# Making every low part of a split operand on VectorE instead of GpSimd, in a two-layer hybrid decoder trunk

## The chip, the cores and the metric

The kernel runs on one core of one Trainium2 chip. The metric is the device time of one execution in microseconds, as a median over runs. Before the change it is 3264.32 us (three runs, 3264.29 to 3269.77 us). The engines are TensorE (PE in the profile, with PEld for its weight loads), VectorE (DVE), ScalarE (ACT), GpSimd (POOL) and SyncE (SP, which here only issues DMAs).

## The reference, cut to what matters

The program computes a decoder trunk of two layers on 1040 tokens (16 meta tokens and a sequence of 1024) of width 1024, in float32. Layer 0 mixes tokens with a gated DeltaNet, layer 1 with an mLSTM, and each is followed by a squared-ReLU MLP of width 4096:

```python
for layer in range(DEPTH):                       # DEPTH = 2
    hn = rms_norm(h, attn_norm[layer])
    mix = gated_deltanet(hn, ...) if layer == 0 else mlstm(hn, ...)
    h = h + mix
    h = h + squared_relu_mlp(rms_norm(h, ffn_norm[layer]), ff_up[layer], ff_down[layer])
return h[:, N_META:]

def gated_deltanet(h, w_in, w_conv, ...):
    proj = h @ w_in                              # 1024 x 6176
    qkv = causal_conv_silu(qkv, w_conv)          # depthwise, 4 taps
    ...                                          # chunked delta rule, 16 heads of 128
    return o.reshape(b, t, GDN_V_DIM).astype(h.dtype) @ w_out

def squared_relu_mlp(h, w_up, w_down):
    a = jax.nn.relu(h @ w_up)
    return (a * a) @ w_down
```

## The kernel before

**Split operands.** Every dense product is made as three matmuls. An operand `x` is split into a high part `hi`, a copy of `x` in the type fp32r that ScalarE makes (a CAST in the profile), and a low part `lo = x - hi`, an elementwise subtraction. `mm3` (lines 115 to 117) then adds `whi*xhi`, `whi*xlo` and `wlo*xhi` into one PSUM bank. So each weight tile and each activation tile costs one CAST on ScalarE and one subtraction on VectorE or GpSimd, and line 117 is the matmul that needs the weight's low part.

**Where low parts are made.** `load_split` (lines 128 to 136) brings a weight tile of 128x1024 (128x768 in part of the mLSTM's output projection) with a DMA into `wraw`, casts it to `whi` (line 134) and subtracts it into `wlo` (line 135) on GpSimd. `wraw`, `whi` and `wlo` have two buffers each. It is called 248 times: for the input and output projections of both mixers and for the down projections of both MLPs. GpSimd also makes: half of the low parts of the first normalised input (`norm_in`, line 312, 10 of 20); every second one of the normalised input of the mLSTM (`apply`, line 986, 8 of 16); the low part of the first three of seven blocks of the MLP's combined input (`combine`, line 1011, 128x780, 16 times, while VectorE makes the other four blocks on line 1013); and, in the up projection, four of the seven low parts of 128x512 (`operand`, line 1064) in jobs whose flag `help` is set. These are the first three and the last two jobs of each MLP, which work on one half of the tokens, so 40 low parts in all.

**Stages.** The DeltaNet runs first (to about 1050 us): for each pair of heads a dense stream of input projections on TensorE (`ps_in`) is woven with the preparation of the pair before (`prep`: 15 steps of shuffle, multiply and subtract on VectorE, lines 621 to 623) and the recurrent scan of the one before that (`scan`: `pks`, `R`, `py`, `S`, lines 752 to 775). The projected column is read by a causal convolution on VectorE (lines 471 and 473). Then come the DeltaNet's output projection (`ps_out`), the up projection (`ps_up`, whose results VectorE adds on line 1075), the down projection (`ps_dn`, added to the residual `hT` on line 1168), the mLSTM (`ps_m`), its output projection (`ps_mo`, added on line 1606), and the second MLP. At the start of each up projection the normalised input is combined (`combine`, lines 1003 to 1013) beside the output projection and the first up jobs.

**What sets the order.** Each engine runs its own instructions strictly in one order, which is fixed when the program is built: a scheduler puts all instructions in order by their place in the program, by their dependences, by when a buffer comes free, and by its own estimate of durations. Moving an instruction from one engine to another therefore also changes the order of others. An instruction at the head of an engine's order that waits holds back all behind it.

GpSimd keeps some small work in either kernel: powers for norms (lines 298, 556, 705, 1569), masks and copies in `prep` (lines 595 to 598, 655, 665), and the history of the convolution (lines 462 and 468).

Of the kernel before, what the change touches and what calls it, by code (L numbers as in the profile page):

```python
# [7 lines left out]
F32 = mybir.dt.float32  # L8
# [116 lines left out]
    return raw.rearrange("p (a b) -> p a b", a=shape[1]) if len(shape) == 3 else raw  # L125


def load_split(c, src, shape, lo_engine=None):
    nc = c.nc
    raw = staging(c, shape)  # L130
    nc.sync.dma_start(out=raw, in_=src)
    hi = c.whl.tile(shape, F32R, tag="whi", name="whi")
    lo = c.whl.tile(shape, F32R, tag="wlo", name="wlo")
    nc.scalar.copy(hi, raw)  # L134
    (lo_engine or nc.gpsimd).tensor_tensor(lo, raw, hi.bitcast(F32), op=ALU.subtract)  # L135
    return hi, lo


# [65 lines left out]
class GDN:  # L204
# [79 lines left out]
    def norm_in(self):  # L284

        nc, c, g2 = self.nc, self.c, self.g2
        self.xh = [c.xact() for _ in range(KT // 2)]
        tags = ("AB", "AB", "V", "V", "sz")
        rows = 112
        spans = [(t0, min(rows, GL[0] - t0)) for t0 in range(0, GL[0], rows)]  # L290
        junk = g2.tile([P, D], F32, tag="sz", name="njunk", bufs=3)
        xs = [self.x_rows(t0, n, g2.tile([P, D], F32, tag=tg, name="nx", bufs=3 if tg == "sz" else 2))
              for (t0, n), tg in zip(spans, tags)]
        for (t0, n), xt in zip(spans, xs):
            ss = self.p2.tile([P, 1], F32, tag="xs1", name="xs1", bufs=len(xs))[:n]
            nc.scalar.activation(junk[:n], xt, AF.Square, accum_out=ss)
            nc.vector.tensor_scalar(ss, ss, 1.0 / D, EPS, op0=ALU.mult, op1=ALU.add)
            nc.gpsimd.tensor_tensor(ss, ss, c.mhalf[:n], op=ALU.pow)
            nc.vector.tensor_scalar(xt, xt, ss[:, 0:1], None, op0=ALU.mult)
        for (t0, n), xn in zip(spans, xs):  # L300
            ts = slice(t0, t0 + n)
            for kk in range(2):
                ks = slice(kk * 4, kk * 4 + 4)
                pn = self.pp.tile([P, 4, P], F32, tag="pp", name="pn")[:, :, :n]
                for j in range(4):
                    nc.tensor.transpose(pn[:, j], xn[:, (kk * 4 + j) * P:(kk * 4 + j + 1) * P], c.ident[:n, :n])
                xw = self.p2.tile([P, 4, rows], F32, tag="raw", name="xw")[:, :, :n]
                nc.vector.tensor_tensor(xw, pn, bc(c.attn_nw[0][:, ks], 2, n), op=ALU.mult)
                for j in range(2):
                    hi, lo = (t[:, :, ts] for t in self.xh[2 * kk + j])  # L310
                    nc.scalar.copy(hi, xw[:, 2 * j:2 * j + 2])
                    (nc.gpsimd, nc.vector)[kk].tensor_tensor(lo, xw[:, 2 * j:2 * j + 2], hi.bitcast(F32),
                                                             op=ALU.subtract)

    def h_init(self, cc):

# [606 lines left out]
class Norm:  # L923
# [46 lines left out]
    def apply(self, hf, pool):  # L970

        nc, c = self.nc, self.c
        self.x[hf] = []
        yield
        yield
        r = yield from self.rms(hf)
        ts = slice(hf * HALF, (hf + 1) * HALF)
        for k in range(KT):
            xn = self.pool.tile([P, HALF], F32, tag="xn", name="nxn", bufs=2)
            nc.vector.scalar_tensor_tensor(xn, c.hT[:, k, ts], self.nw[:, k:k + 1],  # L980
                                           r.rearrange("p a b -> p (a b)"), op0=ALU.mult, op1=ALU.mult)
            if k % 2 == 0:
                self.x[hf].append(pair(pool))
            hi, lo = (x[:, k % 2] for x in self.x[hf][-1])
            nc.scalar.copy(hi, xn)
            (nc.vector, nc.gpsimd)[k % 2].tensor_tensor(lo, xn, hi.bitcast(F32), op=ALU.subtract)
            yield

    def combine(self, hf, pool):

        nc, c = self.nc, self.c
        self.x[hf] = []
        yield
        yield
        r = yield from self.rms(hf)
        ts = slice(hf * HALF, (hf + 1) * HALF)
        for j in range(KT // 2):
            b, t = (x.rearrange("p (a b) -> p a b", b=G) for x in self.stages())  # L1000
            hi, lo = (pool.tile([P, 7, G], F32R, tag=n, name=n) for n in ("xhi", "xlo"))
            for k, out in ((j, b[:, 0:4:3]), (j + 4, b[:, 1:3])):
                nc.vector.scalar_tensor_tensor(out, c.hT[:, k, ts].rearrange("p (a b) -> p a b", b=G),  # L1003
                                               self.nw[:, k:k + 1], r, op0=ALU.mult, op1=ALU.mult)
            nc.vector.tensor_tensor(t[:, 0], b[:, 3], b[:, 0], op=ALU.subtract)
            nc.vector.tensor_tensor(t[:, 2], b[:, 2], b[:, 3], op=ALU.subtract)
            nc.vector.tensor_tensor(t[:, 1], b[:, 2], t[:, 0], op=ALU.subtract)
            nc.vector.tensor_tensor(t[:, 3], b[:, 1], t[:, 1], op=ALU.subtract)  # L1008
            yield
            nc.scalar.copy(hi[:, 0:3], b[:, 0:3])  # L1010
            nc.gpsimd.tensor_tensor(lo[:, 0:3], b[:, 0:3], hi[:, 0:3].bitcast(F32), op=ALU.subtract)  # L1011
            nc.scalar.copy(hi[:, 3:7], t)
            nc.vector.tensor_tensor(lo[:, 3:7], t, hi[:, 3:7].bitcast(F32), op=ALU.subtract)
            self.x[hf].append((hi, lo))
            yield


class Up:
# [17 lines left out]
        nc.sync.dma_start(out=r2, in_=w[:, :, (2 * i + 1) * P:(2 * i + 2) * P])  # L1036
        return r1, r2

    def operand(self, raw, name, help):

        nc, c = self.nc, self.c
        r1, r2 = raw[:2]
        a11, a12, a21, a22 = r1[:, 0:4], r1[:, 4:8], r2[:, 0:4], r2[:, 4:8]

        def sub(out, a, b, op=ALU.subtract):
            nc.vector.tensor_tensor(out, a, b, op=op)  # L1046
            return out
        if name == "s2":
            s3 = self.u1.tile([P, KT // 2, P], F32, tag="s3", name="s3")
            raw.append(sub(s3, a11, a21))  # L1050
            x = sub(a11, a22, s3)
        elif name == "s3":
            x = raw[2]
        elif name == "s1":
            x = sub(a21, a21, a22, ALU.add)
        elif name == "s4":
            x = sub(a12, a12, a11)
        else:
            x = {"a11": a11, "a12": a12, "a22": a22}[name]
        w = c.whl.tile([P, KT, P], F32R, tag=("whi", "wlo")[self.nop % 2], name="uop")  # L1060
        self.nop += 1
        nc.scalar.copy(w[:, 0:4], x)  # L1062
        lo = nc.gpsimd if help and name in ("a12", "s3", "a22", "s4") else nc.vector
        lo.tensor_tensor(w[:, 4:8], x, w[:, 0:4].bitcast(F32), op=ALU.subtract)  # L1064
        return w

    def evac(self, i, hs, name, ps, tmp):
# [33 lines left out]
    def run(self, jobs):  # L1101
# [1 line left out]
        n, ahead = len(self.ORDER), 3  # L1103
        raws, ops = {0: list(self.load(jobs[0][0]))}, {}
        done = 0
        for ji, (i, parts, help, before) in enumerate(jobs):
            if before:
                before()
            hs = slice(parts[0], parts[-1] + 1)
            tmp = {}  # L1110
            for u, (name, xi) in enumerate(self.ORDER):
                while done <= min(ji * n + u + ahead, len(jobs) * n - 1):
                    dj, du = divmod(done, n)
                    ops[done] = self.operand(raws[dj], self.ORDER[du][0], jobs[dj][2])
                    if du == n - 1 and dj + 1 < len(jobs):
                        raws[dj + 1] = list(self.load(jobs[dj + 1][0]))
                    done += 1
                w = ops.pop(ji * n + u)
                ps = self.ps.tile([P, 2, 512], F32, tag="pu", name="ps_up")[:, :, :G]
                for hf in parts:  # L1120
                    for k in range(4):
                        hi, lo = (x[:, xi] for x in self.norm.x[hf][k])
                        mm3(self.nc, ps[:, hf], w[:, k], w[:, 4 + k], hi, lo, k == 0, k == 3)
                    yield
                self.evac(i, hs, name, ps[:, hs], tmp)
# [62 lines left out]
def mlp(c, w_up, w_down, norm, spans, sides, xa, st, acts, after, closed):  # L1188
# [5 lines left out]
    with ExitStack() as ust:  # L1194
# [3 lines left out]
        def first_done():  # L1198
# [3 lines left out]
            down.fetch(0)  # L1202
            for j in range(HB):
                down.load(j)
        jobs = [(i, (0,), True, None) for i in range(e)]
        for i in range(e, n - 2):
            jobs.append((i, (0, 1), False, c.drain if i == e else None))
            if i < 2 * e:
                jobs.append((i - e, (1,), False, None))
            elif i < 2 * e + 2:  # L1210
                jobs.append((n - 2 + i - 2 * e, (0,), False, None))
        jobs += [(i, (1,), True, first_done if i == n - 2 else None) for i in range(n - 2, n)]
        c.weave(up.run(jobs))
    down.open(st, sides[0])
    c.norm_psum(True)
# [541 lines left out]
```

## Time and profile before

| | before |
|---|---|
| median of 3 runs | 3264.32 us |
| the profiled execution | 3269.28 us |
| its span, first to last instruction | 3267.5 us |
| TensorE busy | 3095.0 us (95%) |
| VectorE busy | 1910.2 us (58%) |
| ScalarE busy | 1480.2 us (45%) |
| GpSimd busy | 983.4 us (30%) |
| mean granted TensorE clock | 0.984 of full speed |

Busy times of engines overlap each other; each row is to be read against the span. A busy TensorE is one with a matmul in flight, whether at full pace or not. The difference between its busy time and the span is time in which no matmul was in flight.

### The profile page before, as it was taken

The numbers are of one execution on the slowest core, as the hardware profiler recorded it, in microseconds if no ns is written. First come the engines' busy times: TensorE is split into PE (matmuls) and PEld (weight loads), VectorE is DVE, ScalarE is ACT, GpSimd is POOL, SyncE is SP. The second block draws the span as 40 slices with busy tenths as digits, with TensorE's granted clock in tenths as the row PEclk, the third lists the DMA queues.
The fourth block names the chain that finished last, engine by engine and source line by source line (L and its number), as shares of the span: only waits on it lengthen the run. The fifth ranks groups of instructions, "written<-read, shape, count | busy, mean of one in ns | idle before, by whom it ended". The sixth has DMA issues, their size and how long they took to land. (4 is left out here: it accounts for less than half of the span.)

```text
span 3267.5 us, 66042 instructions
## 1 busy us (share of the span) xinstructions
PE 3095.0 (95%) x26788; PEld 2933.6 (90%) x26788; DVE 1910.2 (58%) x4161; ACT 1480.2 (45%) x3394; POOL 983.4 (30%) x858
## 2 busy tenths in 40 slices
PE   7899999998999997999999998999998899999999
PEld 6888888888889897899999998988897799989998
DVE  6767778777766458776634437223237976553332
ACT  5666666665555433555511114444334555441112
POOL 4544554454444334100222224211124300022222
PEclk9899999999999998999999999999998999999999
DMA  3223223322324642433523322221122244343323
GB/s 98 75 75 88 70 80 88 88 82 76 88 67 134 206 141 73 124 120 116 161 73 98 98 66 72 60 59 51 49 91 72 82 137 123 108 132 98 104 85 97
DMA packets 402224, 311.00 MB, mean 95 GB/s; under 512 B 30175, under 2 KB 366432, under 8 KB 401920
## 3 DMA queue, kind: packets, MB, share of 16 engines
q1 hardware_dynamic: 366320, 272.69, 28.5%
q10 hardware_dynamic: 35600, 34.10, 3.0%
q8 instruction: 211, 3.46, 0.4%
q14 instruction: 93, 0.76, 0.1%
HBM read 248.11 MB, written 58.62 MB: 94 GB/s over the span
## 5 line engine op out<-in xcount | busy, mean ns | idle before, releaser
L135 POOL TENSOR_TENSOR wlo<-wraw,whi 128x1024 fp32r<-128x1024 f32 (+1 forms) x248 | 599.3, 2417 | 1163.4 <-ACT whi L134 1123.6
L115 PE MATMUL ps_up<-xhi,uop 128*128 128x260 f32 x1792 | 512.5, 286 | 27.5 <-ACT uop L1062 8.8
L115 PE MATMUL ps_dn<-act_hi,whi 128*128 128x260 f32 (+1 forms) x1792 | 534.7, 299 | 1.8 <-DVE hT L1168 1.6
L116 PE MATMUL ps_dn<-act_lo,whi 128*128 128x260 f32 (+1 forms) x1792 | 534.6, 298 | 0.0
L117 PE MATMUL ps_dn<-act_hi,wlo 128*128 128x260 f32 (+1 forms) x1792 | 532.0, 298 | 0.1
L117 PE MATMUL ps_up<-xhi,uop 128*128 128x260 f32 x1792 | 510.2, 285 | 8.1 <-DVE uop L1064 7.8
L116 PE MATMUL ps_up<-xlo,uop 128*128 128x260 f32 x1792 | 511.3, 286 | 0.2 <-POOL xlo L1011 0.2
L115 PE MATMUL ps_in<-act_hi,whi 128*128 128x264 f32 (+1 forms) x1536 | 457.1, 298 | 20.2 <-ACT raw L465 12.4
L134 ACT CAST whi<-wraw 128x1024 fp32r<-128x1024 f32 (+1 forms) x248 | 255.9, 1032 | 480.2 <-PE ps_dn L116 361.6
L116 PE MATMUL ps_in<-act_lo,whi 128*128 128x264 f32 (+1 forms) x1536 | 453.0, 295 | 0.0
L1168 DVE TENSOR_TENSOR hT<-hT,ps_dn 128x260 f32<-128x260 f32 (+1 forms) x448 | 204.8, 461 | 424.1 <-PE ps_dn L117 423.7
L117 PE MATMUL ps_in<-act_hi,wlo 128*128 128x264 f32 (+1 forms) x1536 | 451.1, 294 | 0.0
L115 PEld LDWEIGHTS ps_up<-xhi,uop 128*128 128x128 f32 x1792 | 342.6, 191 | 31.9 <-ACT uop L1062 12.5
L117 PEld LDWEIGHTS ps_up<-xhi,uop 128*128 128x128 f32 x1792 | 342.2, 191 | 9.6 <-DVE uop L1064 8.8
L115 PEld LDWEIGHTS ps_dn<-act_hi,whi 128*128 128x128 f32 x1792 | 336.9, 188 | 13.8 <-issue 1.4
L117 PEld LDWEIGHTS ps_dn<-act_hi,wlo 128*128 128x128 f32 x1792 | 337.4, 189 | 11.0 <-POOL wlo L135 0.3
L116 PEld LDWEIGHTS ps_dn<-act_lo,whi 128*128 128x128 f32 x1792 | 337.1, 188 | 10.4
L116 PEld LDWEIGHTS ps_up<-xlo,uop 128*128 128x128 f32 x1792 | 342.6, 191 | 0.5 <-POOL xlo L1011 0.4
L115 PEld LDWEIGHTS ps_in<-act_hi,whi 128*128 128x128 f32 x1536 | 294.5, 192 | 26.3 <-ACT raw L465 14.1
L117 PEld LDWEIGHTS ps_in<-act_hi,wlo 128*128 128x128 f32 x1536 | 294.5, 192 | 4.3 <-issue 1.6
L116 PEld LDWEIGHTS ps_in<-act_lo,whi 128*128 128x128 f32 x1536 | 294.6, 192 | 3.8 <-issue 1.4
L115 PE MATMUL ps_m<-act_hi,whi 128*128 128x260 f32 x768 | 224.2, 292 | 6.8 <-ACT mso L1444 3.7
(419 smaller groups left out, 6845.3 us busy)
## 6 DMA issues: line engine op xcount, KB each, us to landing
wraw<-in_gdn_in_dram SPq DMA_DIRECT2D x96, 512.0 KB
wraw<-in_ff_down_dram SPq DMA_DIRECT2D x72, 512.0 KB
a_st<-d_a SPq DMA_DIRECT2D x64, 520.0 KB
d_a<-up_c ACTq DMA_DIRECT2D x88, 260.0 KB
wraw<-in_ff_up_dram SPq DMA_DIRECT2D x42, 512.0 KB
r<-in_ff_up_dram SPq DMA_DIRECT2D x42, 512.0 KB
wraw<-in_gdn_out_dram SPq DMA_DIRECT2D x32, 512.0 KB
wraw<-in_mlstm_in_dram SPq DMA_DIRECT2D x28, 512.0 KB
```

What stands on the lines that cost most here:

```text
L115: nc.tensor.matmul(ps, whi, xhi, start=first, stop=False)
L116: nc.tensor.matmul(ps, whi, xlo, start=False, stop=False)
L117: nc.tensor.matmul(ps, wlo, xhi, start=False, stop=last)
L134: nc.scalar.copy(hi, raw)
L135: (lo_engine or nc.gpsimd).tensor_tensor(lo, raw, hi.bitcast(F32), op=ALU.subtract)
L1168: nc.vector.tensor_tensor(hT[:, d, t0:t0 + n], hT[:, d, t0:t0 + n], ps, op=ALU.add)
```

## The change

Every low part is subtracted on VectorE. The parameter `lo_engine`, the alternation of engines in `norm_in` and `apply`, and the flag `help` go; GpSimd keeps its small work. 322 subtractions move.

```diff
-def load_split(c, src, shape, lo_engine=None):
+def load_split(c, src, shape):
...
     nc.scalar.copy(hi, raw)
-    (lo_engine or nc.gpsimd).tensor_tensor(lo, raw, hi.bitcast(F32), op=ALU.subtract)
+    nc.vector.tensor_tensor(lo, raw, hi.bitcast(F32), op=ALU.subtract)
     return hi, lo
...
-                    (nc.gpsimd, nc.vector)[kk].tensor_tensor(lo, xw[:, 2 * j:2 * j + 2], hi.bitcast(F32),
-                                                             op=ALU.subtract)
+                    nc.vector.tensor_tensor(lo, xw[:, 2 * j:2 * j + 2], hi.bitcast(F32), op=ALU.subtract)
...
-            (nc.vector, nc.gpsimd)[k % 2].tensor_tensor(lo, xn, hi.bitcast(F32), op=ALU.subtract)
+            nc.vector.tensor_tensor(lo, xn, hi.bitcast(F32), op=ALU.subtract)
...
-            nc.gpsimd.tensor_tensor(lo[:, 0:3], b[:, 0:3], hi[:, 0:3].bitcast(F32), op=ALU.subtract)
+            nc.vector.tensor_tensor(lo[:, 0:3], b[:, 0:3], hi[:, 0:3].bitcast(F32), op=ALU.subtract)
...
-        lo = nc.gpsimd if help and name in ("a12", "s3", "a22", "s4") else nc.vector
-        lo.tensor_tensor(w[:, 4:8], x, w[:, 0:4].bitcast(F32), op=ALU.subtract)
+        nc.vector.tensor_tensor(w[:, 4:8], x, w[:, 0:4].bitcast(F32), op=ALU.subtract)
```

VectorE's order at the start of the DeltaNet, where the input is normalised (`nx`), transposed by TensorE (`pn`), scaled into `xw` and split, and where the first two weight tiles are split. Before:

```order
28 L312 TENSOR_TENSOR act_lo<-xw,act_hi 128x2x112 x2
29 L299 TENSOR_SCALAR nx<-nx,xs_212 80x1024
30 L308 TENSOR_TENSOR xw<-pn,ncols 128x448 x2
31 L312 TENSOR_TENSOR act_lo<-xw,act_hi 128x2x112 x2
32 L308 TENSOR_TENSOR xw<-pn,ncols 128x448 x2
```

and now:

```order
28 L312 TENSOR_TENSOR act_lo<-xw,act_hi 128x2x112 x3
29 L299 TENSOR_SCALAR nx<-nx,xs_212 80x1024
30 L312 TENSOR_TENSOR act_lo<-xw,act_hi 128x2x112
31 L308 TENSOR_TENSOR xw<-pn,ncols 128x448
32 L135 TENSOR_TENSOR wlo<-wraw,whi 128x1024
33 L308 TENSOR_TENSOR xw<-pn,ncols 128x448
34 L135 TENSOR_TENSOR wlo<-wraw,whi 128x1024
35 L312 TENSOR_TENSOR act_lo<-xw,act_hi 128x2x112 x4
36 L308 TENSOR_TENSOR xw<-pn,ncols 128x448 x2
```

The two weight tiles' low parts now stand behind line 299 and around the second `xw`, and each `xw` is followed by four low parts where two stood.

VectorE's order in the mLSTM's output projection, where `combine` for the second MLP runs beside it (`st_b`, `st_t` and `xlo` are `combine`'s, `hT<-hT,ps_mo` frees a PSUM bank of the projection). Before:

```order
2518 L1606 TENSOR_TENSOR hT<-hT,ps_mo 128x260
2519 L1005 TENSOR_TENSOR st_t<-st_b 128x260
2520 L1006 TENSOR_TENSOR st_t<-st_b 128x260
2521 L1007 TENSOR_TENSOR st_t<-st_b,st_t 128x260
2522 L1008 TENSOR_TENSOR st_t<-st_b,st_t 128x260
2523 L1606 TENSOR_TENSOR hT<-hT,ps_mo 128x260
```

and now:

```order
2781 L1604 TENSOR_TENSOR hT<-hT,ps_mo 128x260
2782 L1010 TENSOR_TENSOR xlo<-st_b,xhi 128x780
2783 L1004 TENSOR_TENSOR st_t<-st_b 128x260
2784 L1005 TENSOR_TENSOR st_t<-st_b 128x260
2785 L135 TENSOR_TENSOR wlo<-wraw,whi 128x768
2786 L1604 TENSOR_TENSOR hT<-hT,ps_mo 128x260
2787 L1006 TENSOR_TENSOR st_t<-st_b,st_t 128x260
2788 L1007 TENSOR_TENSOR st_t<-st_b,st_t 128x260
2789 L1604 TENSOR_TENSOR hT<-hT,ps_mo 128x260
```

Between two additions to `hT` there now stand the low part of `combine` and that of a weight tile, and two of `combine`'s own steps have moved behind the second addition.

## Rows read from the trace of the kernel before

**Rows 1.** The page: span; busy us, share and count by engine
```profile
span 3267.5 us, 66042 instructions
PE 3095.0 (95%) x26788; PEld 2933.6 (90%) x26788; DVE 1910.2 (58%) x4161; ACT 1480.2 (45%) x3394; POOL 983.4 (30%) x858
```

**Rows 2.** Windows by stage: length, then each engine's busy us, granted clock, DMA
```profile
0.00:1100.00 1100.00, 1013.16 (x10733) 940.58 (x10734) 791.71 (x2200) 654.68 (x1869) 511.29 (x632) 0.98 0.31 88
1100.00:1350.00 250.00, 216.23 (x1663) 209.50 (x1662) 168.86 (x238) 103.95 (x194) 93.09 (x46) 0.95 0.42 130
1600.00:1950.00 350.00, 347.42 (x2885) 346.79 (x2885) 144.21 (x281) 76.26 (x95) 88.17 (x40) 1.00 0.31 99
1950.00:2050.00 100.00, 89.80 (x711) 86.76 (x710) 66.09 (x86) 40.36 (x80) 46.24 (x24) 0.97 0.25 70
2450.00:2600.00 150.00, 125.61 (x877) 116.81 (x877) 128.35 (x217) 69.89 (x148) 59.88 (x32) 0.90 0.25 75
```

**Rows 3.** Waits of TensorE: who for whom, us in total, times, longest
```profile
PE pks L752 <- DVE S L771: 17.3, 22, 2.3
PE pn L306 <- DVE xw L308: 12.6, 3, 9.9
...
PE ps_out L117 <- POOL wlo L135: 1.6, 2, 1.4
```

**Rows 4.** Costliest groups by line: count, busy us, mean ns, idle before
```profile
L135 POOL TENSOR_TENSOR wlo<-wraw,whi 128x1024 fp32r<-128x1024 f32 (+1 forms) x248 | 599.3, 2417 | 1163.4 <-ACT whi L134 1123.6 <-PE ps_mo L117 14.7 <-PE mpo L1541 7.4
...
L471 DVE TENSOR_SCALAR acc<-raw,ncols 128x528 f32<-128x528 f32 (+1 forms) x64 | 99.6, 1556 | 45.0 <-ACT raw L465 44.7
```

**Rows 5.** Groups of VectorE by shape: busy us, mean ns, idle before
```profile
L1149 DVE TENSOR_TENSOR act_lo<-a_st,act_hi 128x1040 fp32r<-128x1040 f32 x64 | 78.6, 1245 | 17.2 <-ACT act_hi L1148 16.9
...
L1005 DVE TENSOR_TENSOR st_t<-st_b 128x260 f32<-128x260 f32 x16 | 20.2, 1261 | 0.0
```

**Rows 6.** Single lines of VectorE: durations in ns as min/median/max
```profile
L471 DVE TENSOR_SCALAR acc<-raw,ncols x64: 472/1801/2721, 40.6 to 998.0; 128x528 f32<-128x528 f32 x32, 128x512 f32<-128x512 f32 x32
L941 DVE TENSOR_TENSOR ss<-ss,nsq x84: 415/430/2620, 1174.5 to 2547.4; 128x260 f32<-128x260 f32 x84
L1005 DVE TENSOR_TENSOR st_t<-st_b x16: 416/1340/2634, 1224.8 to 2598.8; 128x260 f32<-128x260 f32 x16
L1064 DVE TENSOR_TENSOR uop<-r,uop x74: 677/693/1764, 1281.9 to 2886.2; 128x512 fp32r<-128x512 f32 x74
L1168 DVE TENSOR_TENSOR hT<-hT,ps_dn x448: 410/426/681, 1626.7 to 3261.0; 128x260 f32<-128x260 f32 x148, 128x504 f32<-128x504 f32 x2
```

**Rows 7.** Timeline at the DeltaNet's start: start us, duration us, [idle before]
```profile
15.83 0.75 DVE L299 TENSOR_SCALAR nx<-nx,xs 112x1024 f32<-112x1024 f32 x1
...
18.04 5.74 DVE L299 TENSOR_SCALAR nx<-nx,xs 80x1024 f32<-80x1024 f32 x1
18.60 4.63 POOL L135 TENSOR_TENSOR wlo<-wraw,whi 128x1024 fp32r<-128x1024 f32 x2
...
24.37 1.75 PE L306 MATMUL pn<-ident,nx 112*128 112x112 f32 x8 [9.92 <-DVE xw L308]
```

**Rows 8.** Timeline in the mLSTM's output projection
```profile
2521.51 2.93 POOL L135 TENSOR_TENSOR wlo<-wraw,whi 128x1024 fp32r<-128x1024 f32 x1 [3.21 <-ACT whi L134]
...
2522.47 2.26 DVE L1005 TENSOR_TENSOR st_t<-st_b 128x260 f32<-128x260 f32 x1
2524.41 2.01 POOL L1011 TENSOR_TENSOR xlo<-st_b,xhi 128x780 fp32r<-128x780 f32 x1
2524.66 2.05 DVE L1006 TENSOR_TENSOR st_t<-st_b 128x260 f32<-128x260 f32 x1
...
2527.43 0.59 PE L115 MATMUL ps_mo<-act_hi,whi 128*128 128x260 f32 x1 [4.32 <-DVE hT L1606]
```

**Rows 9.** All waits: VectorE behind ScalarE's casts and copies
```profile
DVE uop L1064 <- ACT uop L1062: 51.8, 55, 2.7
...
DVE acc L471 <- ACT raw L465: 44.7, 32, 3.7
```

More of the change, by code (lines that the diff above doesn't have):

```diff
@@ L1037, in load, with operand @@
         return r1, r2
-    def operand(self, raw, name, help):
+    def operand(self, raw, name):
         nc, c = self.nc, self.c
@@ L1105, in run @@
         done = 0
-        for ji, (i, parts, help, before) in enumerate(jobs):
+        for ji, (i, parts, before) in enumerate(jobs):
             if before:
@@ L1113, in run @@
                     dj, du = divmod(done, n)
-                    ops[done] = self.operand(raws[dj], self.ORDER[du][0], jobs[dj][2])
+                    ops[done] = self.operand(raws[dj], self.ORDER[du][0])
                     if du == n - 1 and dj + 1 < len(jobs):
@@ L1204, in first_done @@
                 down.load(j)
-        jobs = [(i, (0,), True, None) for i in range(e)]
+        jobs = [(i, (0,), None) for i in range(e)]
         for i in range(e, n - 2):
-            jobs.append((i, (0, 1), False, c.drain if i == e else None))
+            jobs.append((i, (0, 1), c.drain if i == e else None))
             if i < 2 * e:
-                jobs.append((i - e, (1,), False, None))
+                jobs.append((i - e, (1,), None))
             elif i < 2 * e + 2:
-                jobs.append((n - 2 + i - 2 * e, (0,), False, None))
-        jobs += [(i, (1,), True, first_done if i == n - 2 else None) for i in range(n - 2, n)]
+                jobs.append((n - 2 + i - 2 * e, (0,), None))
+        jobs += [(i, (1,), first_done if i == n - 2 else None) for i in range(n - 2, n)]
         c.weave(up.run(jobs))
```

## The prediction, made before the changed kernel ran

> **What bounds the kernel now.** I read the page first, then the busy times by stage, then TensorE's waits, then VectorE's instructions by shape and a few stretches of the timeline. The page shows TensorE with a matmul in flight for 3095.0 of 3267.5 us [rows 1], so TensorE is the bound, and all that the other engines can give is the 172.5 us in which it had none, plus what its clock loses. The stages differ [rows 2]. In the first down projection (1600 to 1950 us) TensorE lacks 2.6 us of 350: nothing that VectorE or GpSimd does there matters. TensorE lacks 86.8 us in the DeltaNet (0 to 1100 us), 33.8 in its output projection and the start of the first MLP (to 1350 us), 10.2 between 1950 and 2050 us, and 24.4 between 2450 and 2600 us: 155 of the 172.5 us. In these four stretches the granted clock is also a mix of its two levels, 1.2 and 2.4 GHz: 0.98, 0.95, 0.97 and 0.90 of full speed, which is 22 + 12.5 + 3 + 15 = 52 us of full-speed time. So the question is what TensorE waits for in these four.
>
> It hardly waits for GpSimd: the longest such total is 1.6 us, for weights' low parts [rows 3], though these take 2417 ns each, 599.3 us in all [rows 4]. GpSimd made them early and stood idle 1163.4 us before them. The totals at the head of the list name VectorE (`S` of the scan, 17.3 us; `xw`, 12.6 us) [rows 3]. And VectorE is slow in a way that its shapes do not explain. Line 471, one pass over 512 or 528 elements, takes 1556 ns in the mean, but 472 ns at best and 1801 in the median [rows 4, 6]. Line 941 has a median of 430 ns and a maximum of 2620; line 1005 a minimum of 416 and a median of 1340 [rows 6]. Line 1168, which reads one operand from PSUM, never exceeds 681 ns over 448 instructions [rows 6], although it runs beside GpSimd's low parts in the down projection. The timeline shows what a stretched instruction stands beside: at 18.04 us one of VectorE lasts 5.74 us, while GpSimd makes two low parts in 4.63 us, and ends just behind them [rows 7]; at 2522.47 and 2524.66 us two of 260 elements last 2.26 and 2.05 us, each until a low part on GpSimd ends [rows 8]. VectorE's instructions that read SBUF alone are held while GpSimd subtracts.
>
> **The change part by part: VectorE's account.** Added: 232 low parts of 1024 columns, 16 of 768, 40 of 512, 16 of 780, 8 of 520 and 10 of up to 224. VectorE already makes such subtractions: 1245 ns for 1040 columns [rows 5], 693 for 512 [rows 6], so on a straight line about 1.05 ns a column: 1.23, 0.96, 0.69, 0.97, 0.70 and 0.4 us. That is 285 + 15 + 28 + 16 + 6 + 4 = 353 us. Given back: what GpSimd's subtractions hold. For line 471, 99.6 us less 64 times 0.48 is 69 us [rows 4, 6]; for line 1005, 20.2 less 16 times 0.42 is 13.5 us [rows 5, 6]. The same subtraction over all of VectorE's shapes, each against its own fast tenth (the first in size is line 471's; one with almost nothing is line 1168's, with some 230 between), gives 332 us, of which about 250 fall before 1350 us, 27 between 1950 and 2050 and 36 between 2450 and 2600. The low parts that move into these stretches cost 176, 23 and 27 us there. Of GpSimd's work some stays beside VectorE, so a part of the 332 us stays as well. Its bounds: all goes, or only the share that weights' low parts have of GpSimd's busy time, 599.3 of 983.4, which is 0.61 [rows 1, 4]; I take nine tenths, 300 us, since what stays is short. So VectorE's total comes to 1910 + 353 - 300 = 1963 us, little more than before, but it moves: VectorE gets some 50 us lighter before 1350 us (225 less 176), keeps its load between 1950 and 2050, loses 5 us of it between 2450 and 2600, and gets heavier, by about 5 us in 50, in the down projections. There it is busy 144 of 350 us [rows 2], and TensorE covers it.
>
> **The two places of the order.** At the start, line 299 needs 0.75 us, as the instruction of the same line and length before it took, in place of 5.74; `xw`, for which TensorE waits 9.92 us [rows 7], then stands behind line 299, one more low part and, for its second half, one of a weight (1.23 us): I count 3 to 5 us off the wait, and 2 of these lost again to the extra low parts that follow (six of 0.4 us). In the mLSTM's output projection, between two additions to `hT` stood 2.26 + 2.05 + 0.42 us [rows 8]; now 0.97 + 0.42 + 0.42 + 0.96 = 2.8 us. Of 4.32 us of wait about 1.5 to 2 go. So even where a stretched instruction ends the wait, the new low parts take back half of what is won.
>
> **The sum.** It is made against the profiled execution, 3269.3 us, whose span is 3267.5 us; that execution is 5 us above the median of the runs. First term: TensorE's idle 155 us in the four stretches. The lower bound of what goes is nothing (the new low parts delay as much as the old stretching did), the upper about two fifths (nearly every wait that ends with a stretched instruction of VectorE or with ScalarE behind one). At the two places above a third to a half goes, but most of the waits are short and not of this kind, so I take a fifth: 31 us. Second term, the clock: the granted clock is below full speed in the stretches where TensorE waited, and at 1.00 in the down projection [rows 2]; bounds nothing and two fifths of 52 us; with a fifth of the waits I take a fifth, 10 us. Third term, the new waits of VectorE behind a `whi` that ScalarE has not yet cast, with what is queued behind: the additions that free PSUM, `S` and `R` of the scan. The bounds are nothing and the second rival's price; I take 5 us. The queues of SP are not in the change; a `wraw` buffer comes free earlier by the 1.2 us that VectorE is faster, or later where VectorE is behind, and I count it as nothing: its cover is the second buffer, and without it a late weight would show as TensorE waiting on line 115 for `whi`. The sum is 31 + 10 - 5 = 36 us less: 3233 against the profiled execution, and 3228 us against the median.
>
> A rule that speaks against the change: the Trainium skill, Perfetto Trace Analysis, section Optimizing Scalar/DVE Operations, says that with a saturated DVE it may make sense to offload work, even to GPSIMD, though it adds that the two share an SBUF port and that this might not help. By its first half the sum for 2450 to 2600 us would be a loss; it is the third rival below. By its second half the sum stands, and the stretched rows of this trace [rows 6, 8] are on that side.
>
> **The rivals.** *More comes back.* Once VectorE is on time, ScalarE's copies are too, and the scan's steps come earlier one after the other. Then two fifths of both terms: 62 + 21 - 5 = 78 us, 3187 us. For it: VectorE's own totals are only the head of TensorE's list, and line 465, on ScalarE, shares its queue with activations that wait for the convolution. Against it: many waits are of `S`, 17.3 us in 22 pieces [rows 3], where the recurrence itself is the reason.
>
> *No gain.* VectorE's total is unchanged, and one delay of 1.2 us takes the place of another. Then the time stays within 6.5 us, the 0.2% about which a measurement of this kernel can tell from no change: 3264 us.
>
> *VectorE waits at the head of its order (slower).* GpSimd could wait for `whi` at no price: 1123.6 us [rows 4]. VectorE cannot: its order is strict. The place is the DeltaNet with its output projection, where 128 of the 248 weight tiles are split (96 and 32 by the code) and VectorE is busy 72% of the time (791.71 of 1100) [rows 2]. The nearest rows: line 1064 behind its cast costs 51.8 us over the 254 low parts that VectorE makes there (42 jobs of seven, less 40), 0.20 us each; line 471 behind `raw` 44.7 us over 64, 0.70 us each [rows 9]. At 0.20 the 128 cost 26 us of VectorE's time, less than the 50 that it wins; at 0.70 they cost 90, which is 40 more. It decides from about 0.4 us each. At the upper end TensorE pays perhaps half of the 40 us, VectorE having 28% of its time free there: 20 us more, 3285 us.
>
> *VectorE becomes the bound (slower).* Between 2450 and 2600 us it is busy 128.35 of 150 us [rows 2]. If the port gave nothing back, the 27 us that move in would make 155, and the stretch 5 us longer, and likewise at the start of the first MLP: 3274 us. Against it: lines 1005 and 941, both in this stretch, are the most stretched of all [rows 6].
>
> **How the numbers follow.** The forecast has 0.55, with a range of its own from 3205 to 3250 us; more gain 0.20; no change 0.11; waits at the head 0.10; the bound 0.04. Faster by over 0.2%: 0.75; within: 0.11; slower: 0.14. The range reaches down to the first rival's 3187 and up past the unchanged 3264, and leaves out what is beyond: 3185 to 3268 us.
>
> **What would show it.** Right: line 471 near 480 ns and line 941 near 430 in the mean, VectorE's busy total within 60 us of 1963, GpSimd's under 384 us (983.4 less 599.3), TensorE's idle time in the four stretches down by about 30 us, fewer stretches at the lower clock, and the down projections unchanged in length. Wrong: a long total of VectorE's line 135 waiting for `whi`, `S` or `hT` later than before, or TensorE waiting at line 117 for `wlo`. Were VectorE's stretching to stay without GpSimd's subtractions, the whole account would fall.

## The result, and the profile after

The changed kernel takes 3133.99 us (median of 4 runs, 3129.67 to 3140.2), the kernel before 3265.16 us beside it. The ratio is 0.9597, with a 95% interval of 0.9578 to 0.9616: 131 us faster, where the prediction said 36 and its range began at 3185. The profiled execution takes 3135.46 us. Lines after the first edits have moved by one or two: 471 is 470, 941 is 940, 1005 is 1004, 1168 is 1166, 1606 is 1604.

The page after, span and busy time by engine, against [rows 1]:

```profile
span 3133.5 us, 65556 instructions
PE 3056.0 (98%) x26788; PEld 2910.6 (93%) x26788; DVE 1944.4 (62%) x4483; ACT 1482.9 (47%) x3390; POOL 303.6 (10%) x536
```

The span is 134.0 us shorter. Of these, 95.0 are time with no matmul in flight (172.5 before, 77.5 now), and 39 are time with one in flight. The mean granted clock rose from 0.984 to 0.990 of full speed; taken as what is missing to 1 times the span, the clock's loss fell from 52 us to 31. VectorE's total is 34 us higher than before, and yet TensorE waits less for it.

To see where, both kernels are cut at the same events: the last `ps_in` matmul, the first `ps_up`, `ps_dn`, `ps_m`, `ps_mo`, and so on. Windows of before: length, then busy us (count) of PE, PEld, DVE, ACT and POOL, granted clock, DMA share, GB/s. The stages are the DeltaNet, its output projection, the first down projection and the mLSTM's output projection:

```profile
0.00:1011.80 1011.80, 928.46 (x9725) 862.20 (x9726) 744.58 (x2053) 611.88 (x1743) 474.73 (x592) 0.98 0.30 82
1011.80:1272.10 260.30, 239.93 (x2217) 229.32 (x2216) 148.79 (x287) 107.68 (x243) 104.12 (x71) 0.96 0.48 148
...
1623.70:1998.40 374.70, 371.17 (x3095) 369.91 (x3094) 161.45 (x310) 78.29 (x101) 92.67 (x41) 1.00 0.28 88
...
2395.40:2541.70 146.30, 134.13 (x967) 121.33 (x966) 93.55 (x185) 56.59 (x131) 52.65 (x26) 0.93 0.24 71
```

The same four stages after:

```profile
0.00:925.80 925.80, 899.98 (x9703) 846.10 (x9704) 691.17 (x2127) 609.27 (x1730) 266.06 (x484) 0.99 0.32 90
925.80:1160.50 234.70, 228.86 (x2215) 221.58 (x2214) 150.09 (x351) 108.91 (x249) 20.56 (x36) 0.99 0.52 164
...
1514.30:1883.50 369.20, 368.93 (x3080) 368.61 (x3081) 189.16 (x348) 77.85 (x101) 0.16 (x1) 1.00 0.28 88
...
2275.60:2413.70 138.10, 132.84 (x975) 119.31 (x974) 94.61 (x208) 56.81 (x131) 4.21 (x2) 0.96 0.25 75
```

The DeltaNet gives 86.0 of the 134 us, its output projection 25.6, the mLSTM's output projection 8.2, the other stages 14 together. In the DeltaNet TensorE's idle time falls from 83.3 to 25.8 us. The cuts are made where the next stage's matmuls begin, and after the change two stages overlap: the first `ps_up` runs 3.2 us before the last `ps_out`, the first `ps_m` 1.8 us before the last `ps_dn`. From first to last matmul the output projection is 22.1 us shorter, the first down projection 3.6.

Waits of TensorE (us in total, times, longest). Two of before that [rows 3] does not show:

```profile
PE ps_in L115 <- ACT raw L465: 12.4, 8, 3.6
PE py L722 <- DVE R L757: 11.3, 13, 1.5
```

After, against these and [rows 3]:

```profile
PE pn L306 <- DVE xw L308: 8.6, 4, 5.1
PE ps_up L115 <- DVE up_u L1073: 7.8, 6, 2.2
PE ps_up L117 <- DVE uop L1062: 6.6, 6, 2.0
...
PE ps_mo L115 <- DVE hT L1604: 2.9, 4, 1.1
...
PE pks L751 <- DVE S L770: 1.5, 1, 1.5
```

The wait for the scan's `S`, 17.3 us before, is 1.5 us; that for `raw` is 1.0, and that for `R` is gone. Added up, the waits behind VectorE fell from 104.9 us (90 waits) to 45.4 (44), those behind ScalarE from 52.2 to 19.8. No wait for `wlo` has come in.

Lines of VectorE: first the two of [rows 4] (count, busy us, mean ns, idle before), then single lines against [rows 6] (min/median/max ns):

```profile
L135 DVE TENSOR_TENSOR wlo<-wraw,whi 128x1024 fp32r<-128x1024 f32 (+1 forms) x248 | 299.9, 1209 | 149.3 <-ACT whi L134 146.8 <-ACT o L744 0.9 <-PE po L753 0.7
...
L470 DVE TENSOR_SCALAR acc<-raw,ncols 128x528 f32<-128x528 f32 (+1 forms) x64 | 32.9, 514 | 1.2 <-ACT raw L464 1.2
```

```profile
L470 DVE TENSOR_SCALAR acc<-raw,ncols x64: 475/487/687, 37.2 to 913.3; 128x528 f32<-128x528 f32 x32, 128x512 f32<-128x512 f32 x32
L940 DVE TENSOR_TENSOR ss<-ss,nsq x84: 412/422/432, 1080.0 to 2426.4; 128x260 f32<-128x260 f32 x84
L1004 DVE TENSOR_TENSOR st_t<-st_b x16: 414/421/425, 1132.4 to 2466.7; 128x260 f32<-128x260 f32 x16
```

The convolution's first pass took 1556 ns in the mean and takes 514; the maxima of 2620 and 2634 ns of the other two are 432 and 425. Most of the stretch is gone: by the prediction's measure, each instruction against its shape's fast tenth, VectorE had 331 us of it and has 48. In its place VectorE has 299.9 us of weights' low parts, and waits 146.8 us for `whi` at the head of its order, 136 times; 60.3 us of that, in 55 waits, lie in the DeltaNet and its output projection. The wait of the convolution for `raw`, 44.7 us [rows 9], is 1.2.

The two places of the order. The start (start us, duration us, [idle before]), against [rows 7]:

```profile
17.29 0.75 DVE L299 TENSOR_SCALAR nx<-nx,xs 80x1024 f32<-80x1024 f32 x1 [0.44 <-POOL xs L298]
17.96 0.38 DVE L312 TENSOR_TENSOR act_lo<-xw,act_hi 128x224 fp32r<-128x224 f32 x1
18.26 0.61 DVE L308 TENSOR_TENSOR xw<-pn,ncols 128x448 f32<-128x448 f32 x1
...
18.93 1.01 PE L306 MATMUL pn<-ident,nx 112*128 112x112 f32 x4 [5.12 <-DVE xw L308]
```

Line 299 takes 0.75 us in place of 5.74, and TensorE's wait is 5.12 us in place of 9.92. The mLSTM's output projection, against [rows 8]:

```profile
2384.02 0.42 DVE L1604 TENSOR_TENSOR hT<-hT,ps_mo 128x260 f32<-128x260 f32 x1
...
2386.72 0.42 DVE L1004 TENSOR_TENSOR st_t<-st_b 128x260 f32<-128x260 f32 x1
...
2387.06 0.42 DVE L1005 TENSOR_TENSOR st_t<-st_b 128x260 f32<-128x260 f32 x1
...
2387.40 0.95 DVE L135 TENSOR_TENSOR wlo<-wraw,whi 128x768 fp32r<-128x768 f32 x1
...
2388.27 0.41 DVE L1604 TENSOR_TENSOR hT<-hT,ps_mo 128x260 f32<-128x260 f32 x1
```

The two steps of 2.26 and 2.05 us take 0.42 each; the longest wait for `hT` there is 1.1 us, not 4.32.

### The profile page after: what moved, and what is told of

Its sections match the earlier page's. It is cut to its first block, busy times and chain, and to the rows that moved or that the text cites. A ratio compares the mean times of both kernels' runs of the same rounds, so it can differ in the third digit from the quotient of the medians.

```text
span 3133.5 us, 65556 instructions
## 1 busy us (share of the span) xinstructions
PE 3056.0 (98%) x26788; PEld 2910.6 (93%) x26788; DVE 1944.4 (62%) x4483; ACT 1482.9 (47%) x3390; POOL 303.6 (10%) x536
## 4 chain that ended last, share of the span: by engine, by line
PE 83%; DVE 7%; DMA 5%; ACT 2%; issue 1%; POOL 1%; SPq 0%; POOLq 0%; DVEq 0%; ACTq 0%
PE ps_dn L115 8%; PE ps_dn L116 8%; PE ps_dn L117 8%; PE ps_up L115 5%; PE ps_up L116 5%; PE ps_up L117 5%; PE ps_in L115 5%; PE ps_in L117 5%; PE ps_in L116 5%; PE ps_m L115 3%; PE ps_m L117 3%; PE ps_m L116 3%; PE ps_out L115 2%; PE ps_out L117 2%; PE ps_out L116 2%
## 5 line engine op out<-in xcount | busy, mean ns | idle before, releaser
L116 PE MATMUL ps_in<-act_lo,whi 128*128 128x264 f32 (+1 forms) x1536 | 446.7, 291 | 0.0
L135 DVE TENSOR_TENSOR wlo<-wraw,whi 128x1024 fp32r<-128x1024 f32 (+1 forms) x248 | 299.9, 1209 | 149.3 <-ACT whi L134 146.8
```

What stands on the lines that cost most here:

```text
L116: nc.tensor.matmul(ps, whi, xlo, start=False, stop=False)
L135: nc.vector.tensor_tensor(lo, raw, hi.bitcast(F32), op=ALU.subtract)
```

## The experiments

Each kernel has four runs, taken beside seven of the kernel before (medians of 3264 to 3268 us). "DeltaNet" is the length of that stage in the profiled execution, to the last `ps_in` matmul (before 1011.8, after 925.8), and VectorE its busy time there. Each kernel that adds to the 96 weight tiles of the DeltaNet's input projection does so in `load_w`.

**Which part of the change gives it.** e3_gdn_only is the kernel before with only the low parts of the DeltaNet's input and of the 96 tiles on VectorE; e4_rest_only is the rest of the change alone.

```
-        return load_split(self.c, ..., [P, KT, P])
+        return load_split(self.c, ..., [P, KT, P], self.nc.vector)     # e3, on before
+        return load_split(self.c, ..., [P, KT, P], self.nc.gpsimd)     # e4, on after
```

> The kernel before, with only the low parts of the DeltaNet's input (10) and of its 96 input projection tiles moved to VectorE. Theory A: the DeltaNet's stretch as short as in the changed kernel (about 926 us to the last matmul of its input projections, 86 less than before), the rest as before: 3179 us. Theory B: not less than 3230 us unless the order in that stretch is the cause; if it is, also 3179. The prediction's share (a fifth of the idle time): 3245 us.

> The changed kernel, with only the low parts of the DeltaNet's input and of its 96 input projection tiles back on GpSimd. Theory A: 3217 us, the 48 us that the other stages won, with the DeltaNet's stretch at 1012 us. Theory B: no forecast, since the order differs from both; somewhere between 3134 and 3265. If the two partial changes do not add up to the whole (86 + 48 of 134), something passes from one stage to the other.

e3 takes 3181.61 us (ratio 0.9750, 0.9734 to 0.9766), DeltaNet 925.1; e4 3215.54 us (0.9849, 0.9834 to 0.9864), DeltaNet 1009.6. Both come out as expected. The gains of 85 and 51 us add up to 136, against 131 to 134 for both, so the stages can be studied apart; the following runs change the DeltaNet alone.

**Holds put back.** e1_port, e6_one and e7_eighths are the kernel after with a GpSimd subtraction per tile that nobody reads, of the same 1024 columns in two pieces, in one, and in eight (in one piece the unread result is bf16, in the others float32); e2_queue fills GpSimd's time and reads one column per tile.

```
+    def hold(self, hi):                       # called for each tile
+        h, pool = hi.rearrange("p a b -> p (a b)").bitcast(F32), self.nc.gpsimd
+        for a in (0, 512):                    # e1; e7: range(0, 1024, 128); e6: all at once
+            pool.tensor_tensor(self.scratch, h[:, a:a + 512], h[:, a:a + 512], op=ALU.subtract)
...
+        pool.tensor_copy(self.scratch[:, 0:1], h[:, 0:1])      # e2 in place of these
+        for _ in range(4):
+            pool.memset(self.scratch, 0.0)
```

> The changed kernel, and for each of the 96 weight tiles of the DeltaNet's input projections GpSimd also makes two subtractions of 128x512 of the tile's high part from itself, into a scratch tile that nobody reads. VectorE still makes every low part that is used. Theory A (VectorE's instructions are held while GpSimd reads SBUF): line 470 goes back above 1500 ns in the mean, and the DeltaNet's stretch loses at least the 86 us that it won: 3220 us or more, up to 3290, since VectorE now has both the low parts and the stretching. Theory B (the new order that the scheduler made is the gain): within 15 us of the changed kernel, 3134 us. Theory C (GpSimd's small work no longer queues behind 2.4 us subtractions): about 3200 to 3220 us, as GpSimd's queue is as full as before, but with line 470 near 500 ns.

> As the kernel with the two extra subtractions on GpSimd, but in their place a copy of one column and four memsets of 128x512, about 2.1 us on GpSimd for each of the 96 tiles, which only write. Theory A: at most 20 us above the changed kernel (3134 to 3155 us), with line 470 well under 1000 ns. Theory B: 3134 us within 15. Theory C: about 3200 to 3220 us, as with the subtractions.

> As e1, with one GpSimd subtraction of 128x1024 (hi - hi, in a scratch tile that nobody reads) per DeltaNet weight tile, where e1 had two of 128x512: the same elements, half as many instructions, each twice as long. Theory 'a hold lasts as long as the GpSimd instruction': the convolution's scalar line goes from 815 ns in e1 towards the 1556 of before, and the time rises above e1's 3198, to about 3220. Rival 'the number of elements on GpSimd decides, not the length of a piece': the line stays near 815 ns and the time near 3198.

> As e1, with eight GpSimd subtractions of 128x128 per DeltaNet weight tile in place of two of 128x512: the same elements again, in pieces of a quarter of the length. Theory 'a hold lasts as long as the GpSimd instruction': the convolution's scalar line at 500 to 650 ns, and the time near that of e2, 3145 to 3165. Rival 'the elements decide': near e1's, 815 ns and 3198; many short holds in a row would look the same as a long one.

| | us | ratio, interval | DeltaNet us | VectorE us |
|---|---|---|---|---|
| after | 3133.99 | 0.9597, 0.9578 to 0.9616 | 925.8 | 691.2 |
| e2_queue | 3144.84 | 0.9633, 0.9619 to 0.9648 | 935.1 | 685.3 |
| e7_eighths | 3170.84 | 0.9707, 0.9691 to 0.9724 | 968.4 | 735.5 |
| e1_port | 3198.37 | 0.9797, 0.9774 to 0.9819 | 989.0 | 791.6 |
| e6_one | 3220.45 | 0.9861, 0.9846 to 0.9876 | 1015.0 | 814.8 |

The convolution's first pass (min/median/max ns) in e7, in e1 and in e6:

```profile
L478 DVE TENSOR_SCALAR acc<-raw,ncols x64: 474/610/716, 37.2 to 942.4; 128x528 f32<-128x528 f32 x32, 128x512 f32<-128x512 f32 x32
```

```profile
L478 DVE TENSOR_SCALAR acc<-raw,ncols x64: 472/682/1354, 37.6 to 969.1; 128x528 f32<-128x528 f32 x32, 128x512 f32<-128x512 f32 x32
```

```profile
L477 DVE TENSOR_SCALAR acc<-raw,ncols x64: 473/486/2129, 38.0 to 988.6; 128x528 f32<-128x528 f32 x32, 128x512 f32<-128x512 f32 x32
```

And the GpSimd instruction beside it in each, in the same order:

```profile
L450 POOL TENSOR_TENSOR scratch<-whi x768: 390/402/5573, 17.5 to 945.6; 128x128 f32<-128x128 f32 x192
```

```profile
L450 POOL TENSOR_TENSOR scratch<-whi x192: 1029/1068/6215, 17.5 to 968.2; 128x512 f32<-128x512 f32 x192
```

```profile
L449 POOL TENSOR_TENSOR scratch<-whi x96: 1883/2157/7067, 17.0 to 987.7; 128x1024 bf16<-128x1024 f32 x96
```

The longest pass grows with the GpSimd instruction: 716, 1354 and 2129 ns beside 402, 1068 and 2157 in the median. In e6 43 of the 64 passes stay under 700 ns and the other 21 last over 1500, with none between: a pass is held for long or hardly at all. The Trainium skill, SBUF — State Buffer, section "SBUF: two separate sides", says that the port pair which the two engines share is locked by one of them for the whole instruction, and is not split; these rows agree. The same elements in longer instructions cost more time, 37, 64 and 86 us over after, so the rival of e6 and e7 ("the elements decide") falls. So does another, that the added reads keep the buffers of `whi` busy: ScalarE waits for them 4.8 us in e7, 2.8 in e1 and 2.1 in e6. e2, whose GpSimd is busy for 525 us of the stage (e1: 523), costs only 11, and some of its passes are held too (up to 956 ns, as the last section shows for longer fills): GpSimd's crowded order is a small part. Three sizes were missed: e1 was expected at 3220 us or more with a pass above 1500 ns in the mean (815), and e7 came out 6 us above its interval.

**Work put on VectorE.** e5_twice subtracts each tile's low part twice; e8_aside and e10_half add an unread subtraction on VectorE, at every tile and at every second; e9_before_aside is e8's edit on the kernel before; e11_no_lo has no low part for these tiles (left out of the result: the third matmul reads the high part).

```
+        for _ in range(2):                                                    # e5
+            nc.vector.tensor_tensor(lo, raw, hi.bitcast(F32), op=ALU.subtract)
...
+        self.nc.vector.tensor_tensor(self.scratch, h, h, op=ALU.subtract)     # e8, e9; e10: if col // P % 2
...
+        self.nc.scalar.copy(hi, raw)                                          # e11
+        return hi, hi
```

> The kernel after, with the low part of each of the 96 weight tiles of the DeltaNet's input projection subtracted twice on VectorE, into the same tile: 96 x 1.23 = 118 us more of VectorE's work in the DeltaNet, none of it stretched and all of it known to the scheduler. It tests why the gain was 131 us where 36 were forecast. Theory 'planned work is cheap': 122 us of low parts that the change adds there cost little, because TensorE has other work in the order at such a place; e1 gave 63 us of time for 100 us of stretch (0.63), which with about 175 us of stretch before and 86 us of gain leaves about 0.2 us of time for each us of planned work. Then +24 us: about 3158. Rival 'a us of VectorE is a us of VectorE': a planned us costs as much as a stretched one, 0.63: +74 us, about 3208; then the gain would have another cause than the stretch.

> The kernel after, with one more VectorE subtraction of 128x1024 per DeltaNet weight tile that nobody reads (hi - hi into a scratch tile), beside the low part and not in it: as much extra work as in e5 (96 x 1.2 = 115 us), but off the path of the low part. e5 measured +67 us where the cheap-work theory said +24. Theory 'work on VectorE costs about 0.6 us of time for each us, whatever it is' (then stretch and low parts count alike, and some 50 us of the gain in the DeltaNet must come from something else than VectorE's load): +65 to +75 us, about 3200. Theory 'planned work is cheap, e5's price was the late low part': 0 to +25 us, about 3150.

> The kernel before, with the same unread VectorE subtraction of 128x1024 per DeltaNet weight tile: VectorE gets the work that the change brings it there (96 x 1.2 = 115 us), and GpSimd goes on making the low parts. Theory 'a us is a us': about +70 us, 3335. Theory 'planned work is cheap': +0 to +25, 3265 to 3290. e6, which has VectorE's low parts and as long holds as before, came to 1015 us in the DeltaNet against 1012 before; if e9 costs 70, then making the low part on GpSimd costs some 50 to 70 us by itself, beside the stretch; if it costs nothing, the stretch alone explains before.

> As e8, with the unread VectorE subtraction at every second DeltaNet weight tile only: 48 x 1.2 = 58 us more of VectorE's work than after. e8's 115 us cost 92. Theory 'VectorE's planned work is cheap while the order has room for it and dear beyond' (own work of VectorE in the DeltaNet, unstretched and summed: 751 us after, 862 in e5 and e8; v1 with 819 was no slower than after): +5 to +25 us, 3140 to 3160. Theory 'every us of VectorE costs the same 0.7 to 0.8': +41 to +46, about 3178.

> The kernel after without the 96 low parts of the weights of the DeltaNet's input projection: the third matmul takes the high part again in place of the low part, so as many matmuls run, and 96 x 1.23 = 118 us of VectorE's work go (the low parts of these weights are left out of the result). It measures what the added low parts cost the change in that stage. Theory 'cheap while there is room': 0 to 15 us less than after, 3120 to 3134, and the term that the prediction subtracted for new low parts was far too large. Theory 'every us costs the same': 0.7 x 118 = 83 us less by rate, cut off where TensorE's own 895 us of that stage bind, so 25 to 30 us less, about 3105.

| | us | ratio, interval | DeltaNet us | VectorE us |
|---|---|---|---|---|
| e11_no_lo | 3129.00 | 0.9575, 0.9556 to 0.9594 | 923.4 | 589.0 |
| after | 3133.99 | 0.9597, 0.9578 to 0.9616 | 925.8 | 691.2 |
| e10_half | 3156.57 | 0.9664, 0.9643 to 0.9685 | 954.4 | 732.2 |
| e5_twice | 3200.66 | 0.9804, 0.9790 to 0.9819 | 994.7 | 783.7 |
| e8_aside | 3226.42 | 0.9884, 0.9869 to 0.9899 | 1011.9 | 783.9 |
| before | 3264 to 3268 | 1 | 1011.8 | 744.6 |
| e9_before_aside | 3308.44 | 1.0144, 1.0123 to 1.0165 | 1056.6 | 861.8 |

e5 broke the theory that I had drawn from e1 (work that stands in the order is cheap): 67 us where it said 24. e8 showed that it was not the late low part, since the work beside it costs even more: 92 us, above both of its forecasts. e10 and e11 came out as the theory of room in the order said, and gave a curve: the 102 us of VectorE's time between e11 and after cost 2.4 us of the stage (5 us of the medians, whose intervals overlap), the next 41 us cost 29, and twice as many subtractions 86. For work added at each tile there is a knee, and the changed kernel stands near it. But before, with 745 us, lies far off this curve, which gives about 965 there: some 45 us were still open. Nor was the same work free where the holds were left: in e9 it lengthens the stage by 45 us and the run by 44, between its two forecasts (0 to 25 and 70).

**Holds at a low load.** e12_hold_low is e11 with e6's `hold`; e13_pool_makes is e11 with the low part's tile filled by GpSimd. Both leave these low parts out of the result.

```
+        self.hold(hi)                                           # e12
+        return hi, hi
...
+        pool.tensor_copy(lo[:, 0, 0:1], hi[:, 0, 0:1])          # e13
+        for _ in range(2):
+            pool.memset(lo.bitcast(F32), 0.0)
+        return hi, lo
```

> e11 (no low parts of these 96 weight tiles anywhere; they are left out of the result) with e6's GpSimd subtraction of 128x1024 per tile, which nobody reads: the holds alone, at the VectorE load that the kernel before had. Theory 'the holds cost what the change gave, whatever the load': 60 to 90 us above e11, 3190 to 3220. Theory 'a held us counts like a worked one': VectorE stays near the load of after (589 + 125 = 714 us of busy time against 691), where a us costs about half: 0 to 20 us above e11, 3130 to 3150, and then some 60 us of the stage's gain are not the holds'.

> e11 with what TensorE's third matmul reads made on GpSimd again, without holds: a copy of one column of the high part, and then two fills of 128x1024 with zeros (so the low parts of these weights are left out of the result), some 2.9 us from the cast to the low part, as long as the subtraction on GpSimd took in the kernel before. Theory 'GpSimd as the maker costs by itself' (TensorE's third matmul, and the small work behind in GpSimd's order, come later): 30 to 50 us above e11, 3160 to 3180. Theory 'only the holds cost': as e2 did over after, about 10 us above e11, 3140.

e12 takes 3182.09 us (0.9740, 0.9724 to 0.9757), e13 3142.71 (0.9615, 0.9600 to 0.9630). The DeltaNet in e11:

```profile
0.00:923.40 923.40, 897.99 (x9726) 846.47 (x9727) 589.00 (x2075) 621.38 (x1748) 229.13 (x485) 1.00 0.32 90
```

and in e12:

```profile
0.00:979.40 979.40, 920.11 (x9718) 857.41 (x9719) 696.53 (x2064) 612.55 (x1744) 415.99 (x581) 0.98 0.31 85
```

e12 lies 53 us above e11, between its two forecasts and near the first (60 to 90); e13 lies 14 above, near its second. The pair of after and e12 decides. From e11's 589 us of VectorE, 102 us of low parts lead to after and cost 2.4 us; 107.5 us of holds lead to e12, with nearly the same busy time as after (697 against 691), and cost 56. A held microsecond cost 0.52 of time, a planned one 0.02. TensorE's waits in e12 show where:

```profile
PE pks L761 <- DVE S L780: 13.1, 17, 2.2
```

`S` of the scan is waited for again, 13.1 us against 1.5 after. From e12 to before it is 32 us more in the stage; there VectorE is busy 48 us more, its holds being longer (GpSimd's subtraction takes 2417 ns in the mean [rows 4], e12's 1994), and 48 times 0.52 is 25. The rest, 7 us, and e13's 21 us in the stage bound what the making on GpSimd costs by itself. In e13 GpSimd is busier than in e12 (433 us against 416), and the 21 us are mostly holds too: its fills hold VectorE (last section), which is busy 621 us against e11's 589, and 32 times 0.52 is 17. By the measure of the fast tenth, before has 192 us of stretch in the DeltaNet, e11 30 and e12 144: 162 us of stretch for 88 us of time, and 114 for 56, are 0.54 and 0.49. So the holds account for the stage of before, with no large cost of the making beside them.

**A further step.** v1_prep also moves the masks, additions and copies of `prep` (`bt`, `Bc`, `Uf`, `LP`) from GpSimd to VectorE.

```
-            nc.gpsimd.tensor_copy(Uf[sl, :, sl], U[sl])
+            nc.vector.tensor_copy(Uf[sl, :, sl], U[sl])
```

> The kernel after, with the masks, additions and copies of the DeltaNet's preparation (bt, Bc, Uf, LP) on VectorE too, which leaves GpSimd the powers and the convolution's history. If short GpSimd instructions hold VectorE as the low parts did, the shuffles' neighbours (Dec 382 ns in e2, 554 in e1) lose what is left of their stretch and the waits for Bc go: some 10 to 20 us less, near 3120. If not, some 50 us more of VectorE's work at 0.2 us of time each: about 3144. The sign is open; I expect within 0.5% of 3134.

3131.55 us (0.9590, 0.9575 to 0.9604), DeltaNet 918.8, VectorE 738.4. Its interval and that of after overlap, so it can't be called better; it lies within the expected 0.5% of 3134, and neither price, 3120 nor 3144, is shown. 47 us more of busy time on VectorE cost nothing there, against the 29 that e10 paid for 41. The waits for `Bc` and the last held instructions went with it (line 511: 447 ns in the mean after, 342 here), which I take for the reason. So VectorE's load alone does not set the knee: at 738 us this stage is 36 us shorter than e10's at 732.

## Why the prediction was wrong

Its direction, its place and its mechanism held; the size of the first term failed.

**What held.** The stretch was the holds (e1, e6, e7, e12) and left with GpSimd's subtractions. VectorE's total, 1944.4, is within 19 us of the 1963 of the account, in part by luck: summed by duration the low parts added 328 us, not 353, and all else on VectorE gave back 272, not 300, and the two errors offset each other. Before 1350 us it was to get 50 us lighter; in the DeltaNet and its output projection it got 52 lighter. The lines named came to 514 and 422 ns. GpSimd has 303.6 us, below 384. At the start the wait for `xw` lost 4.8 us, inside the 3 to 5; of these 2 were to be lost again, and the first `ps_in` matmul runs 3.8 us earlier (27.9 to 24.2 us). The new waits were put at 5 us; e11, without the low parts of the DeltaNet's tiles, is 5 us faster in the median, with an interval that overlaps that of after. The second down projection kept its length to 0.4 us; the first became 3.6 us shorter from first to last matmul, nearly all of it idle time, which was not foreseen.

**The step that failed: "most of the waits are short and not of this kind, so I take a fifth: 31 us".** Idle time fell by 95.0 us, more than half of all 172.5, and by 72 in the DeltaNet and its output projection alone. Even the upper bound of two fifths, 62 us, was too low. Two readings led there. First, the 17.3 us of `S` in 22 pieces [rows 3] were put down to the recurrence itself; with the holds gone, 1.5 is left. The 13 short waits for `R` of the same scan went whole. Short waits, many of them, were here the mark of a chain that is held a little everywhere, and not of one that could go no faster. Second, "the new low parts take back half of what is won", read off two places and weighed microsecond for microsecond, was carried into the sum; in the DeltaNet they took back 2.4 us of 88 (from before, 1011.8, to e11, 923.4). At the second place, too, 3.2 us of the 4.32 went, not 1.5 to 2.

**The clock.** 10 us were forecast, about 21 came (52 to 31). It fell with the idle time, as the step said; the share was the same error. Of the 39 us that went with a matmul in flight, the clock can account for 21. The other 18 or more are a term that the sum lacked; no run shows what they are.

**The rivals.** *More comes back* (78 us) had the right mechanism and was still too small. *VectorE waits at the head of its order* is in the trace: 60.3 us for the 128 low parts of the DeltaNet and its output projection, 0.47 us each, just above the 0.4 us from which it was to decide. It did not come true: VectorE was busy 691 of 926 us in the DeltaNet, and without the 96 low parts there (e11) the stage is only 2.4 us shorter. With 48 subtractions more it costs 29 us (e10), and with 96 more the stage is as long as before (e8, 1011.9). *VectorE becomes the bound* did not come: in the mLSTM's output projection it is busy 94.6 us against 93.6, in a stage 8.2 us shorter.

**What stays open.** Why a planned microsecond is so much cheaper than a held one below the knee, and what sets the knee, since v1_prep lies beyond it by load and pays nothing. That the order is made with the low part's duration in it, while a hold falls on whatever comes next, fits e11, e12 and the wait for `S`, but it was only argued: no run here keeps the order and changes the holds alone. For the 48 us outside the DeltaNet only e4 stands, as a whole; that holds are the cause there too is carried over from the stretched lines, and not shown by a run.

## What to carry to other kernels

If an instruction's median is far above its minimum for the same shape (1801 against 472 ns here), look for what holds it, and do not price the hold by its share of busy time. In this kernel, where TensorE is the bound and VectorE feeds it through chains, a held microsecond cost 0.52 of time at a low load of VectorE (e12), and 0.63, 0.72 and 0.96 at a higher one (e1, e6, e7); many short waits for that engine went with the holds.

Price work that is added to the feeding engine apart from its holds: here nearly nothing up to 691 of 926 us, and 0.7 to 0.9 a microsecond for work added at each tile beyond that (e10, e5, e8), where it is no cheaper than a hold. That load is a mark of this kernel and not a rule (v1_prep). If GpSimd must work beside VectorE, short pieces did better here (e7 against e6: 50 us).

## What was not expected of the hardware

Fills on GpSimd, which read no tensor, hold some of VectorE's instructions. In e13 the convolution's first pass, with one tensor operand, beside fills of 128x1024:

```profile
L479 DVE TENSOR_SCALAR acc<-raw,ncols x64: 471/1142/1396, 36.5 to 931.3; 128x528 f32<-128x528 f32 x32, 128x512 f32<-128x512 f32 x32
```

```profile
L450 POOL MEMSET wlo<- x192: 941/952/1245, 18.6 to 932.3; 128x1024 f32 x192
```

The median is 1142 ns against 487 after, the maximum about the pass plus one fill. The subtractions of two tensors in `prep` were not held in the same run: line 631, `U<-U,tm`, 238 ns in the mean to 920 us, against 235 after (before: 297).
